# Attention phase: queries made pair by pair, four buffers of transposed queries, and two scratch tiles moved into other tiles' buffers

## The chip, the core and the metric

The kernel runs on one core of a Trainium2 chip. A core has a matrix engine (TensorE, PE in the views), a vector engine (VectorE, DVE), a scalar engine (ScalarE, ACT), a general engine (GpSimd, POOL) and a sequencer that here does nothing but start DMA transfers (SyncE, SP). Each engine works through its own list of instructions in order; an instruction that is not ready holds up everything behind it on that engine. The metric is the device time of one execution in microseconds (us), lower is better; the median of three runs is given.

## What is computed

One step of a one-layer hybrid decoder: 2048 prompt tokens and 8 x 8 sample tokens of width 1024. The changed part is the prompt's sliding-window attention; the rest (a Mamba-2 branch, gates and output projections) is listed for its place only.

```python
h = rms_norm(x, p['norm_w'])
proj = h @ p['w_in']                        # 1024 -> q | k | v | z_attn | z_ssd | xBC | dt | gates
q = partial_rope(rms_norm(q.reshape(b, L, 16, 64), p['q_norm_w']), pos)
k = partial_rope(rms_norm(k.reshape(b, L, 4, 64), p['k_norm_w']), pos)
o_a = window_attention_prompt(q, k, v, p['sinks'])   # window 128, 4 query heads per key head
...
o_s, new_conv, new_ssm = ssd_branch(...)             # Mamba-2 scan
p_a = (o_a * jax.nn.silu(z_a)) @ p['w_attn_proj']
...
y = x + merged @ p['w_out']
```

## The kernel before

The program has three phases one after the other: T1 (all of the prompt's attention, 0 to about 745 us), S (the Mamba-2 scan) and T2 (output projections, with the sample tokens' part inside). The change touches T1 only.

T1 walks over 4 blocks `b` of 512 tokens, and in each over 2 pairs of key heads. The 512 normalised tokens of a block, transposed, lie in eight tiles `hT` (one for each 128 of the 1024 channels, each as a high and a low part). Weights come by DMA into `raw`, are split into a high and a low part (`whl`: ACT casts at L150, DVE subtracts at L151) and multiplied in three products for each pair of parts (helpers at L186, L199 and L210).

- Pair 0 makes the gate tiles `za` (L186), keys and values (L210), the queries of the pair (`q_tile`), then, in `prep_h`, prepares the next block, and then runs `attn_unit` for the 4 token tiles of 128.
- `prep_h(b+1)` goes by token tile: load x into `xt`, square it on ACT to get the sum (L269, the squares themselves go into `junk` and are never read), the power on POOL (L227, L228), scale on DVE (L274), 8 transposes on PE (L314), split by ACT and DVE into two staging tiles `hst` (one for each half `kh` of the channels, L150 and L151), and 4 stores of 256 KB into DRAM (`h_d`, L318). In block 1 `prep_s` does the same once for the sample tokens (`xsm`, L326, straight into a tile `hs`).
- Pair 1 makes its queries and `za` tiles, loads the next block's 8 `hT` tiles from `h_d` (`load_h`, L333, 512 KB each) and runs its 4 units. Tile `k` of `hT` needs the stores of all four token tiles.
- `attn_unit`: scores `sc` (L541), mask on ACT and DVE (L547, L548), softmax on DVE and ACT with POOL (L380 to L393), transposes `tr` of the probabilities (L558), a product by head halves on DVE into `PT` (L560), the product with the values (L570, into `tr` again), and the gate (L581). After the last unit's L570 the `tr` buffers go to the next pair's query transposes (L515).
- In block 2 the sample tokens' columns are projected too (`sample_cols`, and in `za_tile` with a transpose at L449): result in `zt`, and a DMA to DRAM. `v_tile` puts its `dt` columns into `dtt` (L491), which a DMA carries off.

A list scheduler works the program out before it runs: it sets the order of the rows on each engine by its own estimates. Buffers come from pools with a fixed number per tag, in program order: a tile waits until all readers of the buffer's last tile are done, a DMA that reads it included. In T1: PSUM `mm` 3, `tr` 3, `sc` 2; SBUF `hst` 2, `junk` 1, `zt` 1, `dtt` 1, `qT` 3, `whl` 2.

Of the kernel before, what the change touches and what calls it, by code (L numbers as in the profile page):

```python
# [17 lines left out]
P = 128  # L18
# [60 lines left out]
def build(tc, nc, a, o, seq, phases=("T1", "S", "T2"), dbg=None):  # L79
# [183 lines left out]
        for hl in range(2):  # L263
            late(Dcol[64 * hl : 64 * hl + 64], dv[hl].partition_broadcast(64))

    def norm_x(xt, jp, nwb, n=P):
        st = jp.tile([P, 3], F32, name="rs", tag="rs", bufs=2)[:n]
        junk = jp.tile([P, D], mybir.dt.bfloat16, name="junk", tag="junk")
        A.activation(junk[:n], xt, AF.Square, accum_out=st[:, 0:1])  # L269
        rpow(st[:, 2:3], st[:, 0:1], 1.0 / D, EPS, st[:, 1:2])  # L270
        if nwb is None:
            V.tensor_scalar(xt, xt, st[:, 2:3], None, ALU.mult)
        else:
            V.scalar_tensor_tensor(out=xt, in0=xt, scalar=st[:, 2:3], in1=nwb[:n], op0=ALU.mult, op1=ALU.mult)  # L274

    def prep_first(xp, jp, zap, trp):
        rows = jp.tile([KT, P], F32, name="rows", tag="rows")
        zz = zap.tile([P, HG, TB], F32, name="zs", tag="zs").rearrange("p (i c) t -> p i (c t)", i=2)
        xts = [xp.tile([P, D], F32, name="xt", tag="xt") if tt < 2 else zz[:, tt - 2] for tt in range(NT)]
        for tt, xt in enumerate(xts):  # L280
            SY.dma_start(xt, a["x_prompt"][0, tt * P : (tt + 1) * P, :])
        SY.dma_start(rows, a["norm_w"][0].rearrange("(c p) -> c p", p=P))
        ips = trp.tile([P, KT], F32, name="tr", tag="tr")
        PE.transpose(ips, rows, ident[:KT, :KT])
        nw = jp.tile([P, KT], F32, name="nw", tag="nw")
        V.tensor_copy(nw, ips)
        for xt in xts:
            norm_x(xt, jp, None)
        hT = []
        for k in range(KT):  # L290
            tp = trp.tile([P, TB], F32, name="tr", tag="tr")
            for tt in range(NT):
                PE.transpose(tp[:, tt * P : (tt + 1) * P], xts[tt][:, k * P : (k + 1) * P], ident)
            ht = cur["h"].tile([P, 2, TB], F32R, name="hT", tag="hT")
            A.activation(ht[:, 0], tp, AF.Identity, bias=0.0, scale=nw[:, k : k + 1])  # L295
            V.scalar_tensor_tensor(
                out=ht[:, 1], in0=tp, scalar=nw[:, k : k + 1], in1=ht[:, 0].bitcast(F32),
                op0=ALU.mult, op1=ALU.subtract,
            )
            SY.dma_start(h_d[0][k // 4][:, k % 4], ht.bitcast(F32))  # L300
            hT.append(ht)
        return hT

    def prep_h(b, xp, jp, trp, nwb):
        for tt in range(NT):
            ts = slice(tt * P, (tt + 1) * P)
            xt = xp.tile([P, D], F32, name="xt", tag="xt")
            SY.dma_start(xt, a["x_prompt"][0, b * TB + tt * P : b * TB + (tt + 1) * P, :])
            norm_x(xt, jp, nwb)
            for kh in range(2):  # L310
                tp = trp.tile([P, 4, P], F32, name="tr", tag="tr")
                for k in range(4):
                    c = (4 * kh + k) * P
                    PE.transpose(tp[:, k], xt[:, c : c + P], ident)  # L314
                st = xp.tile([P, 2, 4, P], F32R, name="hst", tag="hst", bufs=2)
                split(st[:, 0], st[:, 1], tp)
                for i in range(2):
                    SY.dma_start(h_d[b][kh][:, :, i, ts], st[:, i].bitcast(F32))  # L318

    def prep_s(xp, jp, trp, nwb):  # L320
        xsm = xp.tile([64, D], F32, name="xsm", tag="xt")
        SY.dma_start(xsm, a["x_sample"].rearrange("b t d -> (b t) d"))
        norm_x(xsm, jp, nwb, 64)
        tp = trp.tile([P, KT, 64], F32, name="tr", tag="tr")
        for k in range(KT):
            PE.transpose(tp[:, k], xsm[:, k * P : (k + 1) * P], ident[:64, :64])  # L326
        V.tensor_copy(hs, tp)
# [67 lines left out]
    def phase_t1():  # L395
        with ExitStack() as es:
# [6 lines left out]
            jp = pool("jp", 1)  # L403
            one = pool("one", 1)
            wk = pool("wk", 2)
            qtp = pool("qtp", 3)
            kvp = pool("kvp", 1)
            zap = pool("zap", 2)
            sp = pool("sp", 5)
# [69 lines left out]
            def v_tile(b, hT):  # L479
                if b == 0:  # L480
                    SY.dma_start(raw_dt, w_in[:, OFF_DT : OFF_DT + 32].rearrange("(k p) c -> p k c", p=P))
                raw, hl = wload([(0, w_in[:, OFF_V : OFF_V + 256])])
                split(hl[:, 0, :, 256:288], hl[:, 1, :, 256:288], raw_dt)
                if b > 0:
                    G.tensor_copy(vT[:, 0], vT[:, 4])
                dtt = wk.tile([P, NT, 32], F32, name="dtt", tag="dtt", bufs=1)
                for tt in range(NT):
                    ps = mmp.tile([P, 288], F32, name="mm", tag="mm")
                    proj_tm(ps, hl, 288, hT, tt)
                    A.copy(vT[:, tt + 1], ps[:, :256])  # L490
                    V.tensor_copy(dtt[:, tt], ps[:, 256:288])  # L491
                SY.dma_start(dt_d[b], dtt)
                if b == NB - 1:
                    SY.dma_start(o["v_win_p"], vT[:, 4])
                if b == sb:
                    sample_cols(raw, lambda t: [(vn_d[:, P * f : P * f + P], t[64 * f : 64 * f + 64]) for f in range(2)])
                    psd = mmp.tile([P, 32], F32, name="mm", tag="mm")
                    for k in range(KT):
                        for f in range(2):
                            PE.matmul(psd[64 * f : 64 * f + 64], hs[:, k], raw_dt[:, k], start=k == 0, stop=k == KT - 1)  # L500
                    V.tensor_copy(dts, psd)

            def q_tile(b, kv, hT, tab):
                raw, hl = wload([(0, w_in[:, kv * 256 : kv * 256 + 256])])
                out = []
                for tp2 in range(2):
                    ps = mmp.tile([P, TB], F32, name="mm", tag="mm")
                    for j in range(2):
                        proj_tm(ps[:, j * 256 : (j + 1) * 256], hl, 256, hT, 2 * tp2 + j)
                    qr = norm_rope(wk, ps, P, 8, tab[:, 2 * tp2 : 2 * tp2 + 2], 0, 2)  # L510
                    tr = trp.tile([P, 2, 2, P], F32, name="tr", tag="tr")
                    for j in range(2):
                        for h in range(2):
                            src = qr[:, 4 * j + 2 * h : 4 * j + 2 * h + 2].rearrange("p a d -> p (a d)")
                            PE.transpose(tr[:, j, h], src, ident)  # L515
                    qT = qtp.tile([P, 2, HG, P], F32R, name="qT", tag="qT")
                    qv = qT.rearrange("p j (h a) t -> p a j h t", a=2)
                    for a in range(2):
                        ra, rb = slice(64 * a, 64 * a + 64), slice(64 - 64 * a, 128 - 64 * a)
                        A.copy(qv[ra, a], tr[ra])  # L520
                        V.tensor_tensor(qv[rb, a], tr[ra], qv[ra, a].bitcast(F32), ALU.subtract)
                    out += [qT[:, j] for j in range(2)]
                if b == sb:
                    sample_cols(raw, lambda t: [(qks_d[:, P * kv : P * kv + P], t)])
                return out

            def attn_unit(b, pair, tt, qTs, zs):
# [74 lines left out]
            for b in range(NB):  # L602
# [3 lines left out]
                for pair in range(2):  # L606
                    zs = zap.tile([P, HG, TB], F32, name="zs", tag="zs")
                    if pair == 0:
                        for hgp in range(2):
                            za_tile(b, pair, hgp, hT, zs)  # L610
                        tab = tables(b)
                        k_tile(b, hT, tab)
                        v_tile(b, hT)
                    qTs = [q_tile(b, 2 * pair + kvl, hT, tab) for kvl in range(2)]
                    if pair == 0 and b + 1 < NB:
                        prep_h(b + 1, xp, jp, trp, nwb)
                        if b + 1 == sb:
                            prep_s(xp, jp, trp, nwb)
                    if pair == 1:
                        for hgp in range(2):  # L620
                            za_tile(b, pair, hgp, hT, zs)
                    if pair == 1 and b + 1 < NB:
                        nxt = load_h(b + 1, False)
                    for tt in range(NT):
                        attn_unit(b, pair, tt, [qTs[0][tt], qTs[1][tt]], zs)
# [733 lines left out]
```

## Time and profile before

| | us |
|---|---|
| median of 3 runs (3134.69 to 3135.13) | 3134.86 |
| the profiled execution | 3134.82 |
| its span in the profile | 3133.0 |
| PE busy in the span | 3054.0 (97%) |
| DVE, ACT, POOL busy | 1927.0, 1379.3, 858.3 |
| granted TensorE clock, mean | 0.993 |

The profiled execution lies 0.04 us from the median, so sums made against it hold for the median too. 1.8 us of its time lie outside the span. PE is the busiest engine by far; what counts is where it stands idle, and which wait ends last there.

### The profile page before, as it was taken

Reading aid. Unit: us, or ns where it says so; the run is one execution under the profiler, and the core shown is the slowest. Engines: PE = TensorE matmul, PEld = TensorE weight load, DVE = VectorE, ACT = ScalarE, POOL = GpSimd, SP = SyncE. Lnnn points to the kernel's source line nnn. Section 1 sums busy time; section 2 is a strip of 40 time slices with the busy share of each in tenths; the row PEclk is TensorE's granted clock in tenths of the full one; section 3 lists DMA queues with packets and bytes.
Section 4 is the critical chain, followed back from the end, with each engine's and each line's share of the span. In section 5 each row is a group of like instructions: output and inputs, shape, how many; then the busy total and the mean of one; then the engine's idle time right before and its main releaser. Section 6 shows DMA issues by size and latency. Waiting matters only on the chain.

```text
span 3133.0 us, 49824 instructions
## 1 busy us (share of the span) xinstructions
PE 3054.0 (97%) x19462; PEld 2626.2 (84%) x19462; DVE 1927.0 (62%) x3142; ACT 1379.3 (44%) x2863; POOL 858.3 (27%) x865
## 2 busy tenths in 40 slices
PE   8999999988999999999999998999999999999999
PEld 7979787977899888888788886888877899999888
DVE  5868767677777776666667665456556644334433
ACT  4656545455655454444455553343333322222321
POOL 2424332332444444444444443000112110000000
PEclk9999999999999999999999999999999999999999
DMA  6635335254667755565565553455655563345443
GB/s 224 187 109 145 115 111 166 69 169 148 229 236 243 264 205 191 208 238 194 193 255 184 209 202 129 151 140 176 211 174 145 174 192 125 102 147 160 137 108 105
DMA packets 377347, 538.03 MB, mean 172 GB/s; under 512 B 32224, under 2 KB 314616, under 8 KB 366856
## 3 DMA queue, kind: packets, MB, share of 16 engines
q1 hardware_dynamic: 377112, 534.85, 52.3%
q8 instruction: 153, 2.51, 0.3%
q14 instruction: 82, 0.67, 0.1%
HBM read 429.58 MB, written 107.30 MB: 171 GB/s over the span
## 4 chain that ended last, share of the span: by engine, by line
PE 82%; DVE 7%; DMA 5%; ACT 3%; issue 1%; POOL 1%; SPq 0%; POOLq 0%; ACTq 0%; DVEq 0%
PE mm L199 51%; PE mm L210 13%; PE mm L186 5%; PE py L903 3%; PE tr L570 2%; DVE whl L151 2%; PE sc L541 1%; DMA raw<-in_w_in_dram 1%; PE st L912 1%; DVE acc L791 1%; DMA v<-v_d 1%; DMA AB<-ac_d 1%; ACT L L886 1%; PE tr L558 1%; ACT whl L150 1%
## 5 line engine op out<-in xcount | busy, mean ns | idle before, releaser
L199 PE MATMUL mm<-hT,whl 128*128 128x512 f32 (+1 forms) x6720 | 1337.6, 355 | 8.3 <-DVE whl L151 2.9
L199 PEld LDWEIGHTS mm<-hT,whl 128*128 128x128 f32 x6720 | 1113.4, 189 | 180.5 <-issue 11.2
L199 PE MATMUL mm<-ot,whl 128*128 128x512 f32 (+1 forms) x2880 | 567.5, 354 | 1.9 <-ACT ot L150 0.8
L199 PEld LDWEIGHTS mm<-ot,whl 128*128 128x128 f32 x2880 | 475.0, 188 | 72.4 <-ACT ot L150 1.7
L151 DVE TENSOR_TENSOR whl<-raw,whl 128x2048 fp32r<-128x2048 f32 (+1 forms) x172 | 368.2, 2146 | 269.4 <-ACT whl L150 267.5
L150 ACT CAST whl<-raw 128x2048 fp32r<-128x2048 f32 (+1 forms) x172 | 298.5, 1746 | 219.3 <-PE mm L199 103.1
L210 PE MATMUL mm<-whl,hT 128*128 128x256 f32 (+1 forms) x2304 | 304.4, 287 | 3.5 <-DVE dtt L491 1.8
L791 DVE SCALAR_TENSOR_TENSOR acc<-cr,cwb,acc 128x512 f32<-128x512 f32 x288 | 275.3, 958 | 51.1 <-ACT acc L786 47.4
L210 PEld LDWEIGHTS mm<-whl,hT 128*128 128x128 f32 x2304 | 287.6, 189 | 9.2 <-issue 5.3
L210 PE MATMUL mm<-whl,ot 128*128 128x256 f32 (+1 forms) x1632 | 204.0, 284 | 0.0
L210 PEld LDWEIGHTS mm<-whl,ot 128*128 128x128 f32 (+1 forms) x1632 | 198.8, 188 | 3.7 <-issue 2.1
L186 PE MATMUL mm<-hT,whl 128*128 128x512 f32 x768 | 192.7, 400 | 3.0 <-ACT hT L295 2.3
L886 ACT ACTIVATE L<-AB,acs 128x128 f32<-128x128 f32 x512 | 157.0, 391 | 82.7 <-DMA AB<-ac_d 81.8
L888 POOL TENSOR_TENSOR L<-L,cbm 128x1024 f32<-128x1024 f32 x64 | 167.3, 2624 | 88.4 <-DVE cbm L877 71.8
L186 PEld LDWEIGHTS mm<-hT,whl 128*128 128x128 f32 x768 | 141.2, 189 | 34.2 <-ACT hT L295 2.7
L858 DVE SCALAR_TENSOR_TENSOR zs<-th,mm 128x512 f32<-128x512 f32 (+1 forms) x80 | 45.7, 577 | 148.8 <-ACT th L857 148.3
L393 POOL TENSOR_SCALAR s<-s,den 128x128 f32<-128x128 f32 x128 | 78.3, 624 | 200.6 <-DVE den L389 136.0
L150 ACT CAST ot<-v 128x512 fp32r<-128x512 f32 x96 | 58.7, 620 | 165.2 <-DVE v L1225 87.5
L857 ACT ACTIVATE th<-mm 128x512 f32<-128x512 f32 (+1 forms) x80 | 40.0, 507 | 179.1 <-PE mm L199 170.3
L386 ACT ACTIVATE s<-s,ng 128x128 f32<-128x128 f32 x256 | 99.9, 394 | 40.9 <-DVE ng L380 33.6
L795 ACT ACTIVATE th<-acc 128x512 f32<-128x512 f32 x96 | 60.2, 627 | 110.7 <-DVE acc L791 110.3
L785 ACT COPY cr<-mm 128x512 f32<-128x512 f32 (+2 forms) x120 | 59.1, 493 | 111.2 <-PE mm L199 87.0
(323 smaller groups left out, 3923.3 us busy)
## 6 DMA issues: line engine op xcount, KB each, us to landing
raw<-in_w_in_dram SPq DMA_DIRECT2D x72, 1024.0 KB
whl<-w_dx SPq DMA_DIRECT2D x24, 2048.0 KB
whl<-w_dz SPq DMA_DIRECT2D x24, 2048.0 KB
hT<-h_d SPq DMA_DIRECT2D x80, 512.0 KB
AB<-ac_d SPq DMA_DIRECT2D x64, 512.0 KB
raw<-in_w_ssd_proj_dram SPq DMA_DIRECT2D x32, 1024.0 KB
whl<-w_dbc SPq DMA_DIRECT2D x12, 2048.0 KB
raw<-in_w_in_dram SPq DMA_DIRECT2D x40, 512.0 KB
```

The lines of the kernel that those rows point to most:

```text
L150: A.copy(hi, src)
L151: V.tensor_tensor(lo, src, hi.bitcast(F32), ALU.subtract)
L186: PE.matmul(ps, hl[:, x, k, c0 : c0 + P], ht[:, y, :], start=first and i == 0, stop=last and i == n - 1,)
L199: PE.matmul(ps, hl[:, x, k, c0 : c0 + P], ht[:, y, lo : lo + n], start=i == 0, stop=i == 3 * len(hT) - 1,)
L210: PE.matmul(ps, ht[:, x, tt * P : tt * P + m], hl[:, y, k, :n], start=i == 0, stop=i == 3 * len(hT) - 1,)
L386: A.activation(s[:, i, :width], s[:, i, :width], AF.Exp, bias=ng[:, i : i + 1], accum_out=den[:, i : i + 1])
L393: G.tensor_scalar(s[:, i, :width], s[:, i, :width], den[:, i : i + 1], None, ALU.mult)
L570: mm_ = PE.matmul(po[64 * kvl : 64 * kvl + 64], vT[:, tt + w, kv * HD : (kv + 1) * HD], PTs[kvl][:, w], start=w == ws[0], stop=w == 1,)
L791: V.scalar_tensor_tensor(out=acc, in0=raw[:, k : k + TB], scalar=cwb[:, k, ct : ct + 1], in1=acc, op0=ALU.mult, op1=ALU.add)
L886: A.activation(L[:, h], AB[:, h], AF.Relu, scale=-1.0, bias=acs[:, hc.start + h : hc.start + h + 1])
L888: G.tensor_tensor(L, L, cbm[:, c].unsqueeze(1).to_broadcast([P, 8, P]), ALU.mult)
L903: PE.matmul(py[64 * hl : 64 * hl + 64, i], src[:, 2 * i + hl], mov[:, 2 * i + hl], start=src is dx, stop=first or src is not dx,)
```

## The change

Three edits, all in T1.

- **Discard of the squares.** `junk` was a bf16 tile in a buffer of its own. It becomes a float32 tile under the tag `hst`, so the two staging buffers now serve three allocations for each token tile, in turn: squares, first half, second half. The squares of the next token tile thus take the buffer of the first half of this one, and wait for its stores.
- **dt columns.** `dtt` takes the tag `zt`, which has one buffer, so `dtt` and all `zt` tiles wait for one another's DMA.
- **Queries.** `q_tile`, called once for each key head, becomes `q_pair`: the weights of both key heads are loaded first, and the loop over token halves is the outer one. `qT` has 4 buffers for 3.

```diff
-    def norm_x(xt, jp, nwb, n=P):
+    def norm_x(xt, xp, jp, nwb, n=P):
         st = jp.tile([P, 3], F32, name="rs", tag="rs", bufs=2)[:n]
-        junk = jp.tile([P, D], mybir.dt.bfloat16, name="junk", tag="junk")
+        junk = xp.tile([P, D], F32, name="junk", tag="hst", bufs=2)
         A.activation(junk[:n], xt, AF.Square, accum_out=st[:, 0:1])
...
-            qtp = pool("qtp", 3)
+            qtp = pool("qtp", 4)
...
-                dtt = wk.tile([P, NT, 32], F32, name="dtt", tag="dtt", bufs=1)
+                dtt = wk.tile([P, NT, 32], F32, name="dtt", tag="zt", bufs=1)
...
-            def q_tile(b, kv, hT, tab):
-                raw, hl = wload([(0, w_in[:, kv * 256 : kv * 256 + 256])])
-                out = []
+            def q_pair(b, pair, hT, tab):
+                ws = [wload([(0, w_in[:, kv * 256 : kv * 256 + 256])]) for kv in (2 * pair, 2 * pair + 1)]
+                out = [[], []]
                 for tp2 in range(2):
-                    ps = mmp.tile([P, TB], F32, name="mm", tag="mm")
...
-                    out += [qT[:, j] for j in range(2)]
-                if b == sb:
-                    sample_cols(raw, lambda t: [(qks_d[:, P * kv : P * kv + P], t)])
+                    for kvl, (raw, hl) in enumerate(ws):
+                        ps = mmp.tile([P, TB], F32, name="mm", tag="mm")
...
+                        out[kvl] += [qT[:, j] for j in range(2)]
+                        if b == sb and tp2 == 1:
+                            kv = 2 * pair + kvl
+                            sample_cols(raw, lambda t: [(qks_d[:, P * kv : P * kv + P], t)])
                 return out
...
-                    qTs = [q_tile(b, 2 * pair + kvl, hT, tab) for kvl in range(2)]
+                    qTs = q_pair(b, pair, hT, tab)
```

The new orders move rows in several places. From L506 on, line numbers of the changed kernel are 1 or 2 higher (L541 becomes L543, L558 L560, L570 L572).

**First place: end of the preparation in block 1, pair 0.** On PE before, the last token tile's transposes (`xt_3141`) stand inside the first `za` products of pair 1 (`mm_3858`, from this block's `hT_1961` to `hT_1975`):

```order
L314 MATMUL tr_3149<-cst_141,xt_3141 128x128 [waits DVE_49]
L314 MATMUL tr_3149<-cst_141,xt_3141 128x128 x3
L186 MATMUL mm_3858<-hT_1961,whl_3853 128x512 x2
L314 MATMUL tr_3159<-cst_141,xt_3141 128x128 [waits DVE_49]
L314 MATMUL tr_3159<-cst_141,xt_3141 128x128 x3
L186 MATMUL mm_3858<-hT_1963,whl_3853 128x512 x3
```

On PE now, they stand behind the last of the four `za` products of pair 1 (`mm_3950`), and what follows is the first product of the next block (`mm_4359`, from `hT_3978`, the next block's first tile out of `h_d`):

```order
L186 MATMUL mm_3950<-hT_1973,whl_3917 128x512 x3
L186 MATMUL mm_3950<-hT_1975,whl_3917 128x512 x3
L314 MATMUL tr_3149<-cst_141,xt_3141 128x128 [waits DVE_49]
L314 MATMUL tr_3149<-cst_141,xt_3141 128x128 x3
L314 MATMUL tr_3159<-cst_141,xt_3141 128x128 [waits PE_49]
L314 MATMUL tr_3159<-cst_141,xt_3141 128x128 x3
L186 MATMUL mm_4359<-hT_3978,whl_4354 128x512 [waits DMAHW0_49,Activation_49]
L186 MATMUL mm_4359<-hT_3978,whl_4354 128x512 x2
L186 MATMUL mm_4387<-hT_3978,whl_4354 128x512 [waits DVE_49]
L186 MATMUL mm_4387<-hT_3978,whl_4354 128x512 x2
L326 MATMUL tr_3177<-cst_141,xsm_3169 128x64 [waits DVE_49,PE_49]
```

On ACT before, the fourth tile's squares (`junk_3144`) run ahead of the third tile's split (`hst_3126`):

```order
L150 CAST hst_3108<-tr_3103 128x512 [waits DMAHW4_49,DMAHW2_49,Activation_49]
L547 COPY s_3277<-sc_3286 128x256
L269 ACTIVATE junk_3144,rs_3143<-xt_3141 128x1024 [waits DMAHW5_49,Activation_49]
L346 ACTIVATE sq_3751<-mm_3702 128x512 [waits PE_49]
L547 COPY s_3318<-sc_3320 128x256 [waits PE_49]
L520 CAST qT_3052<-tr_3047 64x4x128 [waits DVE_49]
```

On ACT now, they run behind it and wait for DMA transfers out of `hst`:

```order
L150 CAST hst_3126<-tr_3121 128x512 [waits DMAHW7_49,DMAHW3_49,PE_49]
L150 CAST hst_3136<-tr_3131 128x512 [waits PE_49]
L439 ACTIVATE th_3947<-mm_3922 128x512 [waits DVE_49,PE_49]
L269 ACTIVATE junk_3144,rs_3143<-xt_3141 128x1024 [waits DMAHW5_49,DMAHW7_49,DMAHW0_49,DVE_49]
L439 ACTIVATE th_3975<-mm_3950 128x512 [waits DVE_49,PE_49]
L150 CAST whl_4442<-raw_4439 128x8x128 [waits DMAHW5_49,DMAHW4_49]
L150 CAST whl_4442<-raw_4439 128x8x128
L150 CAST hst_3154<-tr_3149 128x512 [waits PE_49,Activation_49]
L150 CAST hst_3164<-tr_3159 128x512 [waits DMAHW2_49,DMAHW1_49,PE_49]
L269 ACTIVATE junk_3172,rs_3171<-xsm_3169 64x1024 [waits DMAHW4_49,DMAHW6_49,DVE_49,Pool_49]
```

The transposes of the last tile moved back by some 60 products of 128x512, next to the work that needs what they lead to.

**Second place: start of block 2.** On PE before, two L449 transposes of `zt` tiles have 24 products for `mm_4812` (values of a token tile) between them:

```order
L449 MATMUL tr_4434<-cst_141,zt_4432 128x128 [waits PE_49]
L210 MATMUL mm_4812<-whl_4724,hT_3978 128x288 [waits DVE_49]
L210 MATMUL mm_4812<-whl_4724,hT_3978 128x288 x2
L210 MATMUL mm_4812<-whl_4724,hT_3980 128x288 x3
...
L210 MATMUL mm_4812<-whl_4724,hT_3992 128x288 x3
L449 MATMUL tr_4522<-cst_141,zt_4520 128x128 [waits DVE_49]
```

On PE now, they follow each other, ahead of three of the four value tiles:

```order
L449 MATMUL tr_4434<-cst_141,zt_4432 128x128 [waits PE_49]
L449 MATMUL tr_4522<-cst_141,zt_4520 128x128 [waits DVE_49,PE_49]
L472 MATMUL tr_4604<-cst_141,kd_4602 128x128 [waits PE_49]
L472 MATMUL tr_4604<-cst_141,kd_4602 128x128 x3
L210 MATMUL mm_4758<-whl_4724,hT_3978 128x288 x3
```

The second transpose has lost the products that stood between.

**Third place: end of T1.** On ACT before, two casts of whole 128x2048 weight tiles for the next phase (`whl_8646`, `whl_8786`) stand ahead of the last scaling (L391) of a unit's probabilities (`s_7659`):

```order
L439 ACTIVATE th_8138<-mm_8113 128x512 [waits PE_49]
L150 CAST hT_8607<-hs_159 128x64
L150 CAST hT_8611<-hs_159 128x64
L150 CAST whl_8646<-raw_8643 128x2048 [waits DMAHW4_49,DMAHW3_49]
L150 CAST whl_8786<-raw_8784 128x2048 [waits DMAHW5_49]
L150 CAST hT_8615<-hs_159 128x64
L391 ACTIVATE s_7659<-s_7659,den_7681 128x128 [waits DVE_49,Activation_49]
```

On ACT now, the scaling comes first:

```order
L391 ACTIVATE s_7659<-s_7659,den_7681 128x128 [waits DVE_49,Activation_49]
L391 ACTIVATE s_7659<-s_7659,den_7681 128x128 [waits Activation_49]
L439 ACTIVATE th_8138<-mm_8113 128x512 [waits PE_49]
L150 CAST hT_8607<-hs_159 128x64 [waits DMAHW6_49]
L150 CAST hT_8611<-hs_159 128x64
L150 CAST whl_8646<-raw_8643 128x2048 [waits DMAHW4_49,DMAHW3_49]
```

The two casts moved behind the scaling; on DVE the two halves of their split (L151) moved behind the unit's products into `PT` in the same way.

## Rows read from the trace of the kernel before

**Rows 1.** The page: span, and busy time of the engines.

```profile
span 3133.0 us, 49824 instructions
PE 3054.0 (97%) x19462; PEld 2626.2 (84%) x19462; DVE 1927.0 (62%) x3142; ACT 1379.3 (44%) x2863; POOL 858.3 (27%) x865
```

**Rows 2.** Stretches: length, busy us of each engine (instructions), PE clock, DMA share, GB/s.

```profile
0.00:745.00 745.00, 700.94 (x4848) 596.74 (x4848) 529.25 (x1106) 399.45 (x1144) 246.59 (x312) 0.99 0.45 141
...
100.00:200.00 100.00, 100.00 (x634) 84.87 (x632) 77.36 (x183) 62.52 (x182) 36.07 (x46) 1.00 0.62 190
...
700.00:800.00 100.00, 84.45 (x555) 73.48 (x554) 76.21 (x176) 57.18 (x172) 25.20 (x35) 0.91 0.50 172
```

**Rows 3.** PE's waits from 0 to 745 us: us in total, times, longest.

```profile
PE tr L570 <- DVE PT L560: 14.5, 8, 4.0
PE tr L284 <- DMA rows<-in_norm_w_dram: 9.7, 1, 9.7
```

**Rows 4.** Lines of the preparation: duration in ns (min/median/max), first and last start.

```profile
L269 ACT ACTIVATE junk<-xt x14: 1047/1057/1087, 4.9 to 464.2; 128x1024 bf16<-128x1024 f32 x14
L269 ACT ACTIVATION_READ_ACCUMULATOR junk<-xt x14: 186/196/233, 5.8 to 465.2; 128x1 f32 x14
...
L227 POOL TENSOR_SCALAR rs<-rs x17: 185/192/937, 6.1 to 465.5; 128x1 f32<-128x1 f32 x16, 64x1 f32<-64x1 f32 x1
...
L228 POOL TENSOR_TENSOR rs<-rs,mhalf x17: 534/557/580, 6.4 to 466.6; 128x1 f32<-128x1 f32 x16, 64x1 f32<-64x1 f32 x1
...
L274 DVE SCALAR_TENSOR_TENSOR xt<-xt,rs,nwb x12: 1255/1278/2276, 42.5 to 468.0; 128x1024 f32<-128x1024 f32 x12
...
L150 ACT CAST hst<-tr x24: 565/586/604, 105.4 to 473.9; 128x512 fp32r<-128x512 f32 x24
L151 DVE TENSOR_TENSOR hst<-tr,hst x24: 653/682/693, 107.6 to 478.5; 128x512 fp32r<-128x512 f32 x24
```

**Rows 5.** Timeline (start, us, engine): DMA issues on SP, and ACT rows that waited for transfers.

```profile
117.57 1.58 SPq L318 DMA_DIRECT2D h_d<-hst  x2
...
122.72 0.59 ACT L150 CAST hst<-tr 128x512 fp32r<-128x512 f32 x1 [4.72 <-DMA h_d<-hst]
...
285.35 0.59 SPq L322 DMA_DIRECT2D xsm<-in_x_sample_dram  x1
...
289.28 1.06 ACT L269 ACTIVATE junk<-xsm 64x1024 bf16<-64x1024 f32 x1 [0.36 <-DMA xsm<-in_x_sample_dram]
```

**Rows 6.** Timeline of PE, block 1, pair 0; in brackets the idle time ahead and its end.

```profile
287.12 0.60 PE L314 MATMUL tr<-cst,xt 128*128 128x128 f32 x4
...
319.24 4.33 PE L186 MATMUL mm<-hT,whl 128*128 128x512 f32 x18
...
335.18 1.94 PE L570 MATMUL tr<-PT,vT 128*64 128x512 f32 x8 [1.08 <-DVE PT L560]
```

**Rows 7.** Timeline of PE in the last pair of T1.

```profile
705.52 1.12 PE L541 MATMUL sc<-KTT,qT 128*128 128x256 f32 x8
...
712.45 0.84 PE L558 MATMUL tr<-cst,s 128*128 128x128 f32 x4 [0.36 <-ACT s L391]
```

**Rows 8.** Timeline of PE at the start of block 2.

```profile
404.68 0.33 PE L449 MATMUL tr<-cst,zt 128*128 128x128 f32 x1
...
408.49 0.33 PE L449 MATMUL tr<-cst,zt 128*128 128x128 f32 x1 [0.28 <-DVE zt L447]
```

**Rows 9.** Timeline of PE where block 3's first pair ends.

```profile
686.39 0.84 PE L558 MATMUL tr<-cst,s 128*128 128x128 f32 x4 [2.56 <-ACT s L391]
691.25 3.68 PE L570 MATMUL tr<-PT,vT 128*64 128x512 f32 x8 [4.02 <-DVE PT L560]
...
697.20 0.74 PE L541 MATMUL sc<-KTT,qT 128*128 128x256 f32 x4 [0.95 <-DVE qT L521]
```

**Rows 10.** Timeline of ACT and of DVE at the same place.

```profile
682.19 3.70 ACT L150 CAST whl<-raw 128x2048 fp32r<-128x2048 f32 x2
...
685.03 4.48 DVE L151 TENSOR_TENSOR whl<-raw,whl 128x2048 fp32r<-128x2048 f32 x2
```

More of the change, by code (lines that the diff above doesn't have):

```diff
@@ L287, in prep_first @@
         for xt in xts:
-            norm_x(xt, jp, None)
+            norm_x(xt, xp, jp, None)
         hT = []
@@ L308, in prep_h @@
             SY.dma_start(xt, a["x_prompt"][0, b * TB + tt * P : b * TB + (tt + 1) * P, :])
-            norm_x(xt, jp, nwb)
+            norm_x(xt, xp, jp, nwb)
             for kh in range(2):
@@ L322, in prep_s @@
         SY.dma_start(xsm, a["x_sample"].rearrange("b t d -> (b t) d"))
-        norm_x(xsm, jp, nwb, 64)
+        norm_x(xsm, xp, jp, nwb, 64)
         tp = trp.tile([P, KT, 64], F32, name="tr", tag="tr")
@@ L501, in v_tile @@
                     V.tensor_copy(dts, psd)
-            def q_tile(b, kv, hT, tab):
-                raw, hl = wload([(0, w_in[:, kv * 256 : kv * 256 + 256])])
-                out = []
+            def q_pair(b, pair, hT, tab):
+                ws = [wload([(0, w_in[:, kv * 256 : kv * 256 + 256])]) for kv in (2 * pair, 2 * pair + 1)]
+                out = [[], []]
                 for tp2 in range(2):
-                    ps = mmp.tile([P, TB], F32, name="mm", tag="mm")
[L508 to L521, printed above, removed]
-                    out += [qT[:, j] for j in range(2)]
-                if b == sb:
-                    sample_cols(raw, lambda t: [(qks_d[:, P * kv : P * kv + P], t)])
@@ new lines, in q_pair @@
+                    for kvl, (raw, hl) in enumerate(ws):
+                        ps = mmp.tile([P, TB], F32, name="mm", tag="mm")
+                        for j in range(2):
+                            proj_tm(ps[:, j * 256 : (j + 1) * 256], hl, 256, hT, 2 * tp2 + j)
+                        qr = norm_rope(wk, ps, P, 8, tab[:, 2 * tp2 : 2 * tp2 + 2], 0, 2)
+                        tr = trp.tile([P, 2, 2, P], F32, name="tr", tag="tr")
+                        for j in range(2):
+                            for h in range(2):
+                                src = qr[:, 4 * j + 2 * h : 4 * j + 2 * h + 2].rearrange("p a d -> p (a d)")
+                                PE.transpose(tr[:, j, h], src, ident)
+                        qT = qtp.tile([P, 2, HG, P], F32R, name="qT", tag="qT")
+                        qv = qT.rearrange("p j (h a) t -> p a j h t", a=2)
+                        for a in range(2):
+                            ra, rb = slice(64 * a, 64 * a + 64), slice(64 - 64 * a, 128 - 64 * a)
+                            A.copy(qv[ra, a], tr[ra])
+                            V.tensor_tensor(qv[rb, a], tr[ra], qv[ra, a].bitcast(F32), ALU.subtract)
+                        out[kvl] += [qT[:, j] for j in range(2)]
+                        if b == sb and tp2 == 1:
+                            kv = 2 * pair + kvl
+                            sample_cols(raw, lambda t: [(qks_d[:, P * kv : P * kv + P], t)])
```

## Prediction

> **What bounds the kernel now.** I read the page's head first: PE is busy for 3054.0 of 3133.0 us [rows 1], so time is won or lost only where PE stands idle, runs at the lower clock, or gets more work. The change adds no product. The orders of before and of the change agree on all engines behind T1, but for a few rows, so I looked at T1 alone. Its 745 us hold 700.94 us of PE work, so 44 us of idle time [rows 2], and 9.7 us of those are the start, which the change leaves alone [rows 3]. That is all a better order could win: some 34 us. What it could lose has no such limit. By stretches, the preparation in block 0 (100 to 200 us) has no idle time at all, while the end of T1 (700 to 800 us) has 15.6 us and a granted clock of 0.91 [rows 2]. The list of waits names the products into PT as the most frequent cause (14.5 us in 8 waits) [rows 3]. No wait of PE in T1 goes back to a store of `hst` or a load of `hT`: that is the point to watch.
>
> **Squares in a staging buffer: the chain it makes.** In `prep_h` the squares of tile t+1 now need the buffer that holds the first half of tile t, and so its stores. From the start of one tile's transposes to the next tile's: 4 transposes 0.60 [rows 6], ACT's part of the split 0.59, DVE's part 0.68, the store, then squares 1.06 and the read of their sum 0.20, POOL 0.19 and 0.56, scaling 1.28 [rows 4]. For the store there is a bound from both sides in one place: SP issued two of them between 117.57 and 119.15, and ACT, which waited 4.72 us for one, went on at 122.72 [rows 5]; that is 3.6 us from the end of the issues, 5.2 from their start. The chain is 8.2 to 9.8 us per tile. Between tiles PE has now, in the tight places, 37 products of 128x512 in block 0 and 35 in block 1 at 0.24 (18 in 4.33 us [rows 6]) and 8 transposes of about 1 us: 9.4 to 9.9 us. So the chain itself about fits, and I cost the waits inside it at nothing; if POOL or DVE are late by 2 us, each of some six places loses up to that.
>
> What it does cost is where the last tile lands. It has moved behind the last `za` product, and the next row on PE is the first product of the next block. In block 1 there is nothing between the two. From the start of the last tile's transposes: 0.60 + 0.59 + 0.68, then the store 3.6 to 5.2, then the load of `hT`, which SP issues behind the stores. No row shows PE waiting for that load. The nearest is the load of `xsm`, of half its size: issued at 285.35, awaited by ACT until 289.28 [rows 5], 3.9 us. I bound the load by 3.9 below and by the longest store, 5.2, above. The sum is 9.4 to 12.3 us; PE is busy for the first 1.0. **PE stands idle for 8.4 to 11.3 us; I take 10**, since SP issues the other half's store ahead of the one that is needed. Before, the last transposes stood at 287.12 and the next block's first product inside the row at 319.24 [rows 6], 32 us later, and nothing waited.
>
> The Trainium skill, in SBUF — State Buffer, section "The DMA setup-cost knee", fits a transfer's time as 2 us plus its bytes at 436 GB/s. By it the 256 KB store would be 2.6 us and the 512 KB load 3.2 us, both estimates, and the pause some 7 us. The rows above are longer than this fit, and the sum goes by the rows.
>
> Behind the pause the pair's tail is packed. ACT has two squares in front of a unit's mask copies, and both wait for the last stores. From scores to the next transposes at best 5.8 us pass (8 score products end at 706.64, transposes at 712.45, of which 0.36 was waiting [rows 7]). In the new order the last unit's second head has 8 products of PT with the values, 1.94 [rows 6], and 4 transposes, 0.6, between its scores and its transposes: a gap of 3.3, less what the wait ahead has covered, taken as 2.6. Two products with the values stand right behind their transposes; there PE waits for the DVE product, as in the row with 1.08 us [rows 6]. With 0.9 and 1.4 for the two, against 1.08 before: **+4**. After an idle stretch PE is slow for a while: behind waits of 2.56 and 4.02 us the eight products took 3.68 us [rows 9] for 1.94 [rows 6]. **+2** for the clock behind 10 idle us, with bounds 1 and 4. Block 1 comes to +16.
>
> In block 0 the last transposes are also moved to the end, but two units' transposes, scores and products (about 8.5 us) still stand between them and the next block's first product. Against the 9.4 to 12.3 us less 1.0 that is a wait of 0 to 2.8, of which packed pairs of transposes and products (cover 0 and 1.1 us for a need of 1.3) take 1.3 and 0.3 anyway. **+3.5** for this pair, bounds 1 and 8. In block 2 the pair is packed likewise, with less of the load left uncovered: **+1.5**, bounds 0 and 4.
>
> **dt columns in zt's buffer.** Before, the two L449 transposes stand at 404.68 and 408.49, and the second waited 0.28 in spite of 24 products between [rows 8]: tanh on ACT, a product on DVE, the DMA that empties the one buffer, a copy on DVE take these 3.8 us. Now nothing lies between, so PE has 3.5 us idle here; and `zt` of the key tile and then `dtt` queue behind it on DVE, each for another such DMA, while the values' PSUM buffers wait for `dtt`. Bounds: nothing, if `dtt`'s waits fall on PE work that goes on, to 7 for a second round trip. I take **+3**, as the 3.5 less what PE waited there before.
>
> **Queries and four buffers.** The same products in another order. Both weight tiles are held to the end of the queries; the splits that need the buffers have some 48 products of 128x256 behind them, and I cost this at nothing. It moves the units' chain at the end of block 3's first pair. There ACT's two casts (3.70 us) stood ahead of the scaling, and DVE's two subtracts (4.48) ahead of PT [rows 10]; PE waited 2.56 + 4.02, ran 3.68 for 1.94, and waited 0.95 [rows 9]: 9.3 us. Both weight pieces are now behind. But the same pieces now come before the last pair's query chain on DVE, and the last pair, with no large product work left beside it, is bound by that chain. I give back half: **-4**, bounds -9.3 and 0.
>
> **Sum.** 16 + 3.5 + 1.5 + 3 - 4 = +20. From 3134.8: **3155 us**.
>
> **Rivals.**
> - *The stores and loads land in time, and only the end of T1 changes.* It needs the pause in block 1 to be covered: stores and load together in under 2 us. For it: before, no PE wait goes to them. Against: the two rows of transfers [rows 5] are each longer than that. Without any pause the rest could reach the full 9.3 us at the end of T1: 3125.5, faster. It decides when that gain passes the losses elsewhere, so at losses under 3 us.
> - *Nothing to measure.* The pause is real but half as long (a store and a load that overlap other work, some 5 us), the second place loses nothing, and the end of T1 gives 4 to 6: 3134 to 3140.
> - *Worse.* Each tile's chain runs over by 2 us in six places because POOL and DVE serve the units first, transfers take the upper bounds, and `dtt` costs its second round trip: 20 + 12 + 1.3 + 4 would be +37; about half of it at once gives 3166 to 3172.
>
> The rule for a double buffer, that transfers should overlap compute (Trainium Kernel Development and Optimization, section "Best Practices" of the Trainium skill), speaks against the first edit, which takes a third user into two buffers. What it costs here is the sum above.
>
> **How the numbers follow.** What a measurement can tell from no change is about 0.2%, 6.3 us. My forecast, a pause of 8 us or more in block 1 and a total between 3141 and 3166, has 0.68; worse than that 0.14; nothing to measure 0.13; faster 0.05. Slower by over 0.2% is thus 0.82. The range leaves out the faster rival and parts of the two others: 3139 to 3168.
>
> **What would show it.** Right: in the changed kernel's trace PE has one wait of 8 to 11 us on a DMA into `hT` near 295 us, with a first product of the next block behind it and a granted clock below 1 in that stretch; a wait of about 3 us at an L449; L269 on ACT waiting for `h_d` stores in blocks 0 to 2; no wait of 2.56 and 4.02 at the end of block 3's first pair. S and T2 take as long as before, within 1 us. Wrong: if the `hT` load shows less than 3 us of wait, if more tiles wait in the chain than the last, or if the last pair of T1 keeps the whole 9.3 us.

## The result and the profile after

The changed kernel takes 3180.22 us (median of 4 runs, 3175.58 to 3184.29) against 3134.99 us for the kernel before: 1.014 times as long, 95% interval 1.0127 to 1.0154, so **45 us slower**. The forecast was 20 us slower, 3155 us, with a range of 3139 to 3168. The direction was right; the size was less than half of what came.

The profiled execution is the shortest of the four, with a span of 3173.8 us, so its trace holds 41 of the 45 us. The page's head, against [rows 1]:

```profile
span 3173.8 us, 49816 instructions
PE 3063.6 (97%) x19462; PEld 2632.2 (83%) x19462; DVE 1928.5 (61%) x3142; ACT 1380.5 (43%) x2863; POOL 864.9 (27%) x865
```

The span grew by 40.8 us. The same 19462 matmuls keep PE busy for 9.6 us more, and PE is idle for 31.2 us more. To see where, I cut both traces at the ends of the same units: pair 0 and pair 1 of block 0, pair 0 of block 1, the next three pairs, block 3, and the rest. The kernel before (columns as in [rows 2]):

```profile
0.00:169.10 169.10, 156.37 (x1031) 138.06 (x1032) 109.91 (x204) 85.52 (x193) 54.66 (x75) 1.00 0.66 208
169.10:235.50 66.40, 63.54 (x436) 54.74 (x437) 48.84 (x122) 40.05 (x124) 20.00 (x27) 1.00 0.27 82
235.50:337.10 101.60, 100.52 (x681) 86.76 (x681) 78.85 (x151) 57.27 (x157) 42.95 (x50) 1.00 0.53 159
337.10:594.00 256.90, 249.87 (x1855) 210.78 (x1853) 186.37 (x388) 135.91 (x406) 78.05 (x99) 0.99 0.38 116
594.00:744.90 150.90, 130.54 (x853) 106.29 (x851) 105.26 (x241) 80.70 (x264) 50.94 (x62) 0.94 0.38 122
744.90:3133.00 2388.10, 2353.18 (x14617) 2029.54 (x14615) 1397.81 (x2037) 979.89 (x1719) 611.67 (x553) 1.00 0.55 181
```

The changed kernel, cut at the same units:

```profile
0.00:181.70 181.70, 160.95 (x1038) 140.64 (x1038) 110.44 (x203) 87.44 (x192) 53.98 (x73) 0.99 0.62 194
181.70:254.00 72.30, 65.02 (x431) 56.10 (x430) 50.36 (x122) 37.80 (x124) 23.40 (x27) 0.95 0.24 76
254.00:374.80 120.80, 104.69 (x682) 88.77 (x682) 80.25 (x151) 58.09 (x157) 42.98 (x50) 0.94 0.44 134
374.80:646.90 272.10, 256.81 (x1882) 216.36 (x1882) 188.00 (x390) 136.41 (x408) 80.24 (x101) 0.97 0.36 110
646.90:788.10 141.20, 125.66 (x822) 102.67 (x822) 102.27 (x239) 81.11 (x264) 49.26 (x62) 0.95 0.40 129
788.10:3173.80 2385.70, 2350.43 (x14615) 2027.67 (x14615) 1397.22 (x2037) 979.68 (x1719) 615.00 (x553) 1.00 0.55 181
```

The first number behind the range is the length, the second PE's busy time. The lengths differ by +12.6, +5.9, +19.2, +15.2, -9.7 and -2.4, which sum to 40.8; some 30 matmuls moved from block 3 to the three pairs ahead of it, so +15.2 and -9.7 are best read together. S and T2 are the last row and did not grow. All of the loss lies in blocks 0 to 2, where the next block is prepared.

PE's waits up to 800 us, against [rows 3]:

```profile
PE tr L572 <- DVE PT L562: 19.3, 13, 2.6
PE mm L186 <- DMA hT<-h_d: 10.8, 1, 10.8
...
PE mm L210 <- DVE dtt L491: 3.7, 1, 3.7
PE tr L449 <- DVE zt L447: 3.6, 1, 3.6
```

The load of `hT` and L449 are the two waits that the prediction had worked out one by one, and both came at their size. They are 14 of 41 us, and 9.6 more are slower products. The rest is not one wait but many, none over 4.7 us (the start aside, which is as before). Where part of it starts shows on ACT, whose list for the discard (L269) says what it waited for (us, times):

```profile
  DMA h_d<-hst: 25.9, 9
```

Nine squares wait for stores out of the staging buffers. Before, no square did, but six splits (L150) waited for the same stores:

```profile
  DMA h_d<-hst: 10.7, 6
```

Now no split does. So ACT's stops for stores moved from the splits to the squares and grew by 15.2 us in sum. Here is one of them, in block 0, on ACT, DVE and PE:

```profile
160.40 1.06 ACT L269 ACTIVATE junk<-xt 128x1024 f32<-128x1024 f32 x1 [4.33 <-DMA h_d<-hst]
161.36 0.19 ACT L269 ACTIVATION_READ_ACCUMULATOR junk<-xt 128x1 f32 x1
161.45 0.62 ACT L549 COPY s<-sc 128x256 f32<-128x256 f32 x2
...
161.84 0.44 DVE L550 COPY_PREDICATED s<-cst,sc 128x256 f32<-128x256 int32 x1 [4.36 <-ACT s L549]
...
162.34 1.61 PE L543 MATMUL sc<-KTT,qT 128*128 128x256 f32 x8 [2.36 <-DVE s L550]
```

The square stands in ACT's list ahead of the mask copies of an attention unit. ACT stops 4.33 us for a store; the copies come behind it; DVE waits 4.36 us for them; the score buffers stay full, and PE waits 2.36 us. The square itself is early work for block 2. What costs here is the wait ahead of it.

### The profile page after: what moved, and what is told of

The parts are those of the page before. It is cut to its first block, busy times and chain, and to the rows that moved or that the text cites. A ratio compares the mean times of both kernels' runs of the same rounds, so it can differ in the third digit from the quotient of the medians.

```text
span 3173.8 us, 49816 instructions
## 1 busy us (share of the span) xinstructions
PE 3063.6 (97%) x19462; PEld 2632.2 (83%) x19462; DVE 1928.5 (61%) x3142; ACT 1380.5 (43%) x2863; POOL 864.9 (27%) x865
## 4 chain that ended last, share of the span: by engine, by line
PE 70%; DVE 5%; DMA 4%; ACT 2%; issue 1%; POOL 0%; SPq 0%; POOLq 0%; DVEq 0%; ACTq 0%
PE mm L199 51%; PE mm L210 7%; PE py L905 4%; PE st L914 1%; PE mm L186 1%; DVE whl L151 1%; DVE acc L793 1%; DMA v<-v_d 1%; PE tr L572 1%; DMA AB<-ac_d 1%; PE tr L896 1%; ACT L L888 1%; PE sc L543 1%; ACT whl L150 0%; DVE PT L562 0%
## 5 line engine op out<-in xcount | busy, mean ns | idle before, releaser
L151 DVE TENSOR_TENSOR whl<-raw,whl 128x2048 fp32r<-128x2048 f32 (+1 forms) x172 | 367.6, 2142 | 263.3 <-ACT whl L150 262.5
L150 ACT CAST whl<-raw 128x2048 fp32r<-128x2048 f32 (+1 forms) x172 | 298.4, 1746 | 212.4 <-PE mm L199 103.1
L393 POOL TENSOR_SCALAR s<-s,den 128x128 f32<-128x128 f32 x128 | 85.6, 680 | 192.4 <-DVE den L389 156.8
L150 ACT CAST ot<-v 128x512 fp32r<-128x512 f32 x96 | 58.7, 620 | 163.6 <-DVE v L1227 87.0
L893 DVE TENSOR_TENSOR AB<-AB,CT 128x1024 f32<-128x1024 f32 x60 | 96.7, 1611 | 20.9 <-ACT AB L892 20.9
```

The lines of the kernel that those rows point to most:

```text
L150: A.copy(hi, src)
L151: V.tensor_tensor(lo, src, hi.bitcast(F32), ALU.subtract)
L393: G.tensor_scalar(s[:, i, :width], s[:, i, :width], den[:, i : i + 1], None, ALU.mult)
L893: V.tensor_tensor(AB, AB, CT[:, sl].unsqueeze(1).to_broadcast([P, 8, P]), ALU.mult)
```

## The experiments

Each ratio is to runs of the kernel before on the same chip, whose median was 3134.99 us for the first row and 3139 to 3140 us for runs 1 to 12; 0.1% is 3.1 us. The scheduler works each of these kernels out anew, so an edit acts through the order of the rows as well as through its waits.

| run | discard | dt columns | queries, qT buffers | ratio (95%) |
|---|---|---|---|---|
| changed kernel | staging, 2 buffers | with zt | pair, 4 | 1.0140 (1.0127 to 1.0154) |
| 1 | staging, 2 | own | by head, 3 | 1.0144 (1.0128 to 1.0160) |
| 2 | own | with zt | by head, 3 | 1.0030 (1.0017 to 1.0042) |
| 3 | own | own | pair, 3 | 0.9987 (0.9977 to 0.9997) |
| 4 | with sq | with zt | pair, 4 | 1.0097 (1.0082 to 1.0112) |
| 5 | staging, 2 | with zt | pair, 3 | 1.0138 (1.0115 to 1.0161) |
| 6 | staging, 3 | with zt | pair, 3 | 1.0069 (1.0051 to 1.0087) |
| 7 | with sq | own | pair, 3 | 1.0048 (1.0031 to 1.0066) |
| 8 | with sq | with tab0 | pair, 4 | 1.0068 (1.0053 to 1.0084) |
| 9 | own, stores twice | own | by head, 3 | 1.0059 (1.0044 to 1.0074) |
| 10 | staging 2, stores twice | own | by head, 3 | 1.0262 (1.0248 to 1.0276) |
| 11 | own, float32 | with zt | pair, 3 | 1.0018 (1.0009 to 1.0027) |
| 12 | own | own, zt 2 buffers | pair, 3 | 0.9970 (0.9961 to 0.9980) |

My theory was that the discard in the staging buffers makes ACT and the preparation wait for stores. The rival was that the new order of the queries packs the preparation at the end of its pair, whatever buffer the discard has.

**Each edit alone (runs 1 to 3).** The discard alone:

```diff
-        junk = jp.tile([P, D], mybir.dt.bfloat16, name="junk", tag="junk")
+        junk = xp.tile([P, D], F32, name="junk", tag="hst", bufs=2)
```

> The kernel before with the first edit alone: the squares' discard in a buffer of the staging tag, the queries and dt columns as before. Discard theory (ACT stops in its list for the stores, and the preparation comes late): +20 to +40 us over before, ACT waiting for h_d stores 15 us or more in L269, and a wait of PE on the hT load of 5 us or more in block 1. Order theory (the queries made pair by pair pack the preparation at the end of the pair, whatever buffer the discard has): within 8 us of before.

It took 1.0144, +45 us: as much as the whole change. The load wait is there (us, times, longest):

```profile
PE mm L186 <- DMA hT<-h_d: 12.7, 5, 10.9
```

ACT waited only 10.7 us for stores in L269, 5 times, less than the 15 expected. No split waited for one, so in sum ACT waited for stores exactly as long as in the kernel before, and yet the time came in above the top of the forecast (+40). The length of ACT's stops does not measure the loss: where they stand in its list counts, and something else about sharing may cost as well. The rival is out: the old order of the queries was in this kernel. The dt columns alone:

```diff
-                dtt = wk.tile([P, NT, 32], F32, name="dtt", tag="dtt", bufs=1)
+                dtt = wk.tile([P, NT, 32], F32, name="dtt", tag="zt", bufs=1)
```

> The kernel before with the second edit alone: the dt columns share the buffer of the sample columns. Both theories: +2 to +7 us, seen as a wait of PE near the L449 transposes or the L491 copies at the start of block 2. If the edit is hidden: within 1 us.

1.0030, +9.4 us, above the range. The wait at L449 is there as worked out, with two waits right ahead of it (PE's timeline):

```profile
397.29 2.50 PE L558 MATMUL tr<-cst,s 128*128 128x128 f32 x8 [2.71 <-ACT s L391]
401.11 3.57 PE L570 MATMUL tr<-PT,vT 128*64 128x512 f32 x8 [1.32 <-DVE PT L560]
404.60 0.33 PE L449 MATMUL tr<-cst,zt 128*128 128x128 f32 x1
408.51 0.45 PE L449 MATMUL tr<-cst,zt 128*128 128x128 f32 x1 [3.58 <-DVE zt L447]
408.75 1.06 PE L472 MATMUL tr<-cst,kd 128*128 128x128 f32 x4
```

and the granted clock of that stretch (columns as before, the clock third from the end):

```profile
400.00:410.00 10.00, 5.32 (x16) 2.43 (x17) 2.52 (x5) 0.71 (x3) 0.05 (x1) 0.67 0.10 33
```

The eight products with the values at 401.11 took 3.57 us for 1.94 at full clock [rows 6]. The whole stretch, between the same two products with the values in both kernels (first the kernel before, then run 2; columns as before):

```profile
390.40:481.50 91.10, 88.06 (x780) 81.19 (x782) 61.24 (x115) 41.81 (x111) 28.90 (x37) 0.98 0.40 117
392.60:491.70 99.10, 90.47 (x778) 82.24 (x780) 61.80 (x115) 43.34 (x111) 28.85 (x37) 0.95 0.37 108
```

It is 8.0 us longer: PE is busy for 2.4 us more and idle for 5.6 us more. The queries alone, with three buffers (a fourth has no room while the discard and the dt columns have their own), `q_pair` as in the change:

> The third edit alone, with three buffers of transposed queries as before (a fourth does not fit beside a discard and dt columns with buffers of their own). Discard theory: -8 to +5 us against before, with no wait of PE on hT. Order theory: +20 us or more.

0.9987, -4 us, as the discard theory had it. Of the two waits at the end of block 3's first pair one of 1.32 us was left, and one of 4.67 us for the query chain on DVE came behind it.

**Another buffer for the discard, and the fourth qT (runs 4 and 5).**

```diff
-        junk = xp.tile([P, D], F32, name="junk", tag="hst", bufs=2)
+        junk = wk.tile([P, D], mybir.dt.bfloat16, name="junk", tag="sq", bufs=1)
```

> The changed kernel with four buffers and the shared dt columns, but the discard in bf16 in the buffer of the query squares (sq, 2 KB, read by DVE and by no DMA). Discard theory: 25 to 45 us faster than the changed kernel, so -8 to +8 us against before; L269 waits for no store, and PE does not wait on hT. Order theory: as slow as the changed kernel, within 8 us.

1.0097: only 14 us faster than the changed kernel, a miss for my theory as it stood. No square waited for a store, and the load of `hT` was not waited for; but L314 now waited for the scaling on DVE four times, 5.7 us. So something else about sharing costs.

```diff
-            qtp = pool("qtp", 4)
+            qtp = pool("qtp", 3)
```

> The changed kernel with three buffers of transposed queries in place of four. Discard theory (two staging buffers for three tiles cost the time): as slow as the changed kernel, +35 to +55 us over before. If the fourth buffer itself costs: 10 us or more faster than the changed kernel.

1.0138: the fourth buffer neither costs nor gains what can be measured.

**What about sharing costs (runs 6 and 11).** Three staging buffers:

```diff
-        junk = xp.tile([P, D], F32, name="junk", tag="hst", bufs=2)
+        junk = xp.tile([P, D], F32, name="junk", tag="hst", bufs=3)
...
-                st = xp.tile([P, 2, 4, P], F32R, name="hst", tag="hst", bufs=2)
+                st = xp.tile([P, 2, 4, P], F32R, name="hst", tag="hst", bufs=3)
```

> As the run before it, with three staging buffers for the three tiles of a token tile, so that squares follow squares in one buffer, which no DMA reads. Discard theory: what is left is the dt columns (+10) and the queries (-4): 0 to +12 us over before, no wait of PE on hT, no wait of L269 on a store. If a float32 discard or its place in the staging pool costs by itself: +25 us or more.

1.0069, above the range. Against run 5 the third buffer gives back 0.69%, 22 us (by the two intervals, some 9 either way), and its L269 waited for no store; PE still waited for `hT`, 2.8 us in five places. But 22 us over before are more than the dt columns and the queries explain. The order on ACT suggested why. With three shared buffers, the squares of the second tile stand behind both splits of the first, and those of the third behind the splits of the second (ACT's timeline in block 0; the first tile's squares ran at 39.63):

```profile
106.88 0.59 ACT L150 CAST hst<-tr 128x512 fp32r<-128x512 f32 x1
108.51 0.58 ACT L150 CAST hst<-tr 128x512 fp32r<-128x512 f32 x1
108.98 1.07 ACT L269 ACTIVATE junk<-xt 128x1024 f32<-128x1024 f32 x1
...
114.12 0.59 ACT L150 CAST hst<-tr 128x512 fp32r<-128x512 f32 x1 [1.90 <-PE tr L314]
116.92 0.56 ACT L150 CAST hst<-tr 128x512 fp32r<-128x512 f32 x1
117.38 1.06 ACT L269 ACTIVATE junk<-xt 128x1024 f32<-128x1024 f32 x1
```

In the kernel before, whose discard has a tag of its own, the squares of two tiles (at 40.26 and 41.80) stand ahead of the first split (105.43), and so on through the preparation. So I gave the same float32 discard its own tag:

```diff
-        junk = xp.tile([P, D], F32, name="junk", tag="hst", bufs=3)
+        junk = xp.tile([P, D], F32, name="junk", tag="junk", bufs=1)
```

> As the run with three staging buffers (which was 22 us over before although no square waited for a store), but with the same float32 discard under a tag of its own. Turn theory: under a shared tag a discard gets its buffer only behind the splits of the token tile before it, so the squares lose their lead of one or two tiles; with a tag of its own the lead is back, and 0 to +10 us over before are left for the dt columns and the queries. If float32 or the pool costs: +17 to +27 us, as with three staging buffers.

1.0018, +5.6 us, as the turn theory had it. The lead is back:

```profile
40.08 1.06 ACT L269 ACTIVATE junk<-xt 128x1024 f32<-128x1024 f32 x1 [2.00 <-DMA xt<-in_x_prompt_dram]
...
41.62 1.05 ACT L269 ACTIVATE junk<-xt 128x1024 f32<-128x1024 f32 x1
...
107.70 0.59 ACT L150 CAST hst<-tr 128x512 fp32r<-128x512 f32 x1
```

It is worth 0.51%, 16 us (some 6 either way). A tag hands out its buffers in the order of the program; a tile that shares it takes its turn behind tiles that have nothing to do with it.

**Discard in sq again, dt columns elsewhere (runs 7 and 8).** Run 7 is run 3 with the discard in `sq`:

> Queries made pair by pair with three buffers and dt columns of their own, as in the third run, but the discard in the buffer of the query squares. If sharing that one buffer with a tile that DVE reads is what kept the fourth run slow: +10 to +28 us over before, with L314 waiting for the scaling on DVE. If the fourth run was slow for its four query buffers: within 6 us of the third run, -8 to +3 us against before.

1.0048, 19 us over run 3, with L314 waiting 5.5 us for the scaling: run 4 was slow for this sharing, not for its four buffers. That the turn behind the query squares is the reason fits, but was not tried by itself: in block 0 the first squares of run 7 ran at 96.70 us, not near 41 as in run 3, though still ahead of the first split (110.31). Run 8 is run 4 with

```diff
-                dtt = wk.tile([P, NT, 32], F32, name="dtt", tag="zt", bufs=1)
+                dtt = wk.tile([P, NT, 80], F32, name="dtt", tag="tab0", bufs=1)[:, :, :32]
```

> The fourth run with the dt columns in the buffer of the rotation tables as loaded (tab0, dead by then) and no longer in that of the sample columns. If the dt edit adds to the rest, as alone (+10): 6 to 13 us faster than the fourth run, +15 to +26 us over before, with no wait of 3 us or more at L449. If it is covered there: within 3 us of the fourth run.

1.0068, 9 us less than run 4: the dt edit costs the same 9 us there, and PE waits for no `zt` at L449.

**Stores made twice (runs 9 and 10).**

```diff
-                for i in range(2):
-                    SY.dma_start(h_d[b][kh][:, :, i, ts], st[:, i].bitcast(F32))
+                for rep in range(2):
+                    for i in range(2):
+                        SY.dma_start(h_d[b][kh][:, :, i, ts], st[:, i].bitcast(F32))
```

> The kernel before with each store of a staging tile made twice, the same bytes to the same place. It prices the stores where no discard shares their buffers. If the stores have slack there: within 10 us of before. If they are tight already (ACT waited 10.7 us for them in six splits): +10 to +25 us.

1.0059, +18.5 us: even the kernel before has no room for a second store. It shows as a new wait of PE for `hT`, 7.4 us in block 0, and not on ACT, whose splits waited 6.9 us for stores where they had waited 10.7. The doubled stores also add traffic for every other transfer; how much of the 18.5 us comes from that was not tried apart.

> The first run (discard in the staging tag alone) with each store made twice. Discard theory, by the wait for the stores: two more stores ahead of each release, some 1 to 3 us each time on the chain of a tile, so 12 us or more over the first run and more than twice what the doubling adds to the kernel before. If the loss is in the order alone and not in the wait for stores: what the doubling adds to the kernel before, within 5 us.

1.0262, 37 us over run 1, far over the 12 expected, and just twice what doubling costs without the shared discard; the intervals leave open whether it is more than twice. It fits that the time of a store is paid once for the split and the load of `hT`, and once more for the squares, but the doubled traffic would have to be told apart from it. That the loss lies in the order alone is out: 37 is not within 5 us of 18.5. In L269 ACT waited

```profile
  DMA h_d<-hst: 34.8, 8
```

34.8 us in 8 squares, against 10.7 in run 1, and one L314 waited 16.4 us for its scaled tile.

**A version that is faster than both (run 12).** Run 3 with two buffers for `zt`:

> The third run (queries pair by pair, three buffers, discard and dt columns with buffers of their own) with two buffers for zt. The small waits at L449 and behind it go: -2 to -8 us against before. If zt's one buffer costs nothing there: as the third run, -4.

0.9970 (0.9961 to 0.9980): 9 us faster than the kernel before, a little beyond the forecast, and 53 us than the changed one. PE waits for no `zt` at L449 there. In run 3 it waited only 0.8 us there, and the intervals of the two runs touch, so what the second buffer itself is worth is not shown.

## Why the prediction was off

By its own steps, against the segments above:

- **Pause in block 1, +10.** Right in kind and in size. PE waited 10.77 us for the load of `hT`, with the next block's first product behind it:

```profile
328.65 1.98 ACT L150 CAST whl<-raw 128x1024 fp32r<-128x1024 f32 x2
330.53 1.07 ACT L150 CAST hst<-tr 128x512 fp32r<-128x512 f32 x2
332.00 1.28 DVE L151 TENSOR_TENSOR hst<-tr,hst 128x512 fp32r<-128x512 f32 x2
335.64 4.21 SPq L333 DMA_DIRECT2D hT<-h_d  x8
339.76 2.90 PE L186 MATMUL mm<-hT,whl 128*128 128x512 f32 x6 [10.77 <-DMA hT<-h_d]
```

  That the size fits so well is partly luck. The last transposes began at 327.96. Two weight casts stood ahead of the split on ACT and their subtracts ahead of it on DVE, so the first half was split only at 332.7, 4.7 us behind that start, where the sum has 1.9. In return the store took 3.0 us to the issue of the load, less than the lower bound of 3.6; the load took 4.1. The place, "near 295 us", was a slip: the next block's first product stood at 319.24 [rows 6], 93 products of 128x512 behind the last transposes (not some 60, as under "The change").

- **Tail of that pair, +4, and clock, +2.** Waits of 1.56, 2.31 and 1.32 us against 1.08 before make +4.1. The stretch from 330 to 350 us has the clock at 0.68 and then 0.81:

```profile
330.00:340.00 10.00, 0.24 (x1) 0.27 (x2) 4.80 (x6) 3.79 (x7) 2.42 (x4) 0.68 0.83 256
340.00:350.00 10.00, 10.00 (x47) 7.89 (x48) 5.64 (x9) 2.39 (x11) 0.00 (x0) 0.81 0.95 374
```

  In this segment PE's busy time rose by 4.2 us for the same work, where I had taken 2 with a bound of 4. The segment came to +19.2 for my +16.
- **"So the chain itself about fits, and I cost the waits inside it at nothing."** This is the step that failed. I had 8.2 to 9.8 us for a tile and 9.4 to 9.9 of cover. The sum was wrong to begin with: the terms named there add up to 8.8 to 10.4, as the 0.56 us of POOL were left out, and so the upper bound did not fit. The trace after has 11.2 us from one L314 (137.39) to the next (148.62):

```profile
137.39 1.03 PE L314 MATMUL tr<-cst,xt 128*128 128x128 f32 x8
138.02 1.07 ACT L150 CAST hst<-tr 128x512 fp32r<-128x512 f32 x2 [0.49 <-PE tr L314]
138.89 1.94 SPq L318 DMA_DIRECT2D h_d<-hst  x3
139.57 1.28 DVE L151 TENSOR_TENSOR hst<-tr,hst 128x512 fp32r<-128x512 f32 x2
145.17 1.06 ACT L269 ACTIVATE junk<-xt 128x1024 f32<-128x1024 f32 x1 [3.08 <-DMA h_d<-hst]
147.28 1.28 DVE L274 SCALAR_TENSOR_TENSOR xt<-xt,rs,nwb 128x1024 f32<-128x1024 f32 x1 [4.47 <-POOL rs L228]
148.62 1.09 PE L314 MATMUL tr<-cst,xt 128*128 128x128 f32 x8 [1.60 <-DVE xt L274]
```

  DVE began its part 1 us late, and the store landed 4.3 us after the three issues ended, where my bounds were 3.6 from the end of the issues and 5.2 from their start. But the wait of PE at L314 is only 0.76 and 1.60 us in block 0 (by my own list, a wait at more tiles than the last was a sign of being wrong). The larger mistake was to ask only whether PE would wait for this chain. ACT waits in it too, 25.9 us, and ACT's list also holds the mask copies and exponentials of the attention units. I had named that for the end of block 1 and priced it nowhere else. Block 0 came to +18.5 us in its two pairs for my +3.5. PE's new waits in pair 0 come to 8.3 us: 2.4 at L314, 2.4 behind the square shown above, and 3.6 in the units now packed behind the last tile. In pair 1 its two longest waits, 2.69 and 3.71 us, each stand behind a weight subtract of 2.28 us on DVE; no store shows in them.
- **The lead of the squares.** No term of the sum. My chain has each tile's squares behind the stores of the tile before, and I took their new place, `junk_3144` behind `hst_3136`, for a consequence of that wait; runs 6 and 11 show that taking turns by itself costs 16 us, without any wait for a store.
- **dt columns, +3.** The wait at L449 was right at 3.6 us. The whole is 9 us (runs 2 and 8), beyond my upper bound of 7. In run 2 the waits in this place are 2.71, 1.32 and 3.58 us, where the kernel before has 0.49, 0.98 and 0.28, and 2.4 us of slower products come on top; in the changed kernel the clock from 440 to 450 us is 0.66.
- **End of T1, -4.** Right in kind: the waits of 2.56 and 4.02 [rows 9] became one of 1.32, and one of 4.66 us for the query chain came. Run 3 has -4 for the queries as a whole.
- **The clock as a whole.** I had +2 for it, once. Busy time rose by 9.6 us, in each of the segments of blocks 0 to 2.

Of the rivals, *Worse* came, and by more than it allowed: 3180 is 8 us over its top of 3172, which was all of its +37 at once (half of its extra 17 would have been 3163). The reason is another in part. The store and the load behind the pause stood below and near my lower bounds, and `dtt` waited 1.6 us for its second round trip on DVE without stopping PE; the tiles' chain, the lost lead and ACT made it. Runs 5, 6 and 11 split the 43 us of run 5: 22 go with the third staging buffer, 16 with the turn, and 5.6 are left for the dt columns and the queries (alone: +9 and -4). How the 22 divide between ACT's stops and the late `hT` was not tried apart. Open, too, is why four executions of the changed kernel lie 8.7 us apart, with granted clocks of 0.987 to 0.989, while those of the kernel before lay within 3 us on that chip.

The Trainium skill, in Trainium Kernel Development and Optimization, section "Best Practices", says that consistent bubbles can mean that SBUF ran out. This case agrees in part: the edits give up 2.5 KB of buffers in each partition and add a fourth `qT`, and the bubbles are the nine stops at L269. But the fourth `qT` gained nothing (run 5), so the room was not needed.

## What to carry to other kernels

A scratch tile that nobody reads is not free in a shared buffer: it takes its turn behind the tiles that share the tag (16 us here), and it waits for the slowest reader of each, here a DMA store. So give a discard a buffer that no DMA reads and that comes round at least as early as its own work does, and price the wait on the engine that would stand still, with everything in that engine's list behind it, and not only on the busiest engine. When a stall is worked out, add the slow products that follow it; in this kernel 31 us of new idle time brought 10 us of slower matmuls.

## What was not expected of the hardware

A group of short waits slowed the products behind it as much as one long wait: behind waits of 2.71 and 1.32 us in run 2 eight products with the values took 3.57 us for 1.94, 1.6 us more, and behind the single wait of 10.77 us in the changed kernel six products of 128x512 took 2.90 us for 1.44 at 0.24 each, 1.5 us more. Stores of 256 KB, which the profile before showed as a wait of ACT of 10.7 us in six splits, cost 18.5 us of device time when each was made twice, while that wait fell to 6.9 us: a wait that shows on one engine does not price the transfer.
